# Plain block products for the first feature pair of the SwiGLUs behind the two mixers

## The chip, the cores and the metric

One core of one Trainium2 chip runs the whole program. The metric is the device time of one execution in microseconds (us), median of several runs. The engines are TensorE (PE in the profile; PEld are its weight loads), VectorE (DVE), ScalarE (ACT), GpSimd (POOL) and SyncE (SP), which issues most transfers.

## What is computed

Two layers work on 560 tokens (512 + 32 + 16, feature-major, so a tile is 128 features by tokens). Layer 0 mixes by gated linear attention (GLA), layer 1 by multi-head latent attention (MLA, 544 of the tokens at its end), and each mixer stands between two half-step SwiGLUs:

```python
def swiglu_half(h, norm_w, w_gate, w_up, w_down):
    hn = rmsnorm(h, norm_w)
    return h + 0.5 * ((jax.nn.silu(hn @ w_gate) * (hn @ w_up)) @ w_down)

for i in range(DEPTH):
    h = swiglu_half(h, ffn1_norm[i], ...)
    h = h + mixer_i(rmsnorm(h, mix_norm[i]))      # GLA in layer 0, MLA in layer 1
    h = swiglu_half(h, ffn2_norm[i], ...)
```

The width is 1024, the inner width of a SwiGLU 2816 = 22 tiles of 128 features.

## The kernel before

**Precision.** A float32 operand is split in a high part (`whi`, ScalarE's cast, L371) and a low part (`wlo`, VectorE's subtraction, L372), and a product is three matmuls: high by high (L415), low by high (L416), high by low (L418).

**A pair of feature tiles.** Gate and up of a SwiGLU go over the 22 feature tiles in 11 pairs. A pair is a product of 2 x 2 blocks: the weights of two tiles (each gate and up) by two halves of the input features, times the two halves of the 1024 input features (row blocks 0 to 3 and 4 to 7 of `h`) by the two halves of the tokens (`b11`, `b12`; `b21`, `b22`). Taken plainly this is eight block products of 24 matmuls. `gate_up` does it in seven, in the manner of Strassen and Winograd: it needs sums of the operand blocks (`t4` to `t7`, beside `b11`, `b21` and `b22`) and of the weight quadrants (`Weights.sums`, three additions of 128 x 1024, and one more in the pair; L290), seven splits of weights instead of four, and copies of partial products (L517). The operand sums are made once and serve all pairs of a SwiGLU that use the form. `plain_gate_up` does the eight products. It is used for the first two pairs of the very first SwiGLU (`plain` is 2 there, then 1), where nothing has been made yet: the first of them makes the plain operands, and in the gaps of the second `combine` makes the sums `t4` to `t7`.

**From mixer to SwiGLU.** At each mixer's end stands its output projection: 16 outputs of `ps` (8 row blocks x 2 halves of the tokens, in the order `Quads.ORDER`: for each i the row blocks i and 4 + i of the first half, then of the second), 12 matmuls each, with three banks `ps` in PSUM. VectorE adds each output to `h` (L760 in GLA, L1412 in MLA), which frees the bank. After each addition the object of the coming SwiGLU, a `Quads`, is called with its row block and half: `parts` scales `h` by the norm's weights and splits it (`scaled_parts`, L181 and L182) and makes the operand sums (L192 to L203 and the splits on `t` and `q`), `square` adds up squares for the norm (L213, L217, L220), and at three counts it loads the first pair's weights, splits two quadrants and makes the weight sums (`ahead`). I call these 16 outputs the mixer's tail. Then comes the first pair: banks A, B, C (two PSUM banks each), the norm's roots (`roots2`: matmuls with ones, L467; steps on `ry`, `rt` on VectorE, L482 to L490; transposes, L475), and `finish` for each feature tile and half (multiply by the root, silu, product, split into `ah` and `al`).

**Order.** The code is written in one order, and the framework's scheduler sets each engine's queue from it by its own estimate; engines run their queue in order and wait for each other by semaphores. In what follows an instruction's line is that of the profile, and the changed kernel's lines are higher by 3 ahead of `plain_gate_up` and by 4 to 6 behind it (L290 becomes L293, L598 L602, L760 L765).

Of the kernel before, what the change touches and what calls it, by code (L numbers as in the profile page):

```python
# [33 lines left out]
HALF_T = ((0, T // 2), (T // 2, T))  # L34
HALF_Q = ((0, TQ // 2), (TQ // 2, TQ))
# [60 lines left out]
class Normed(list):  # L96
# [7 lines left out]
    def parts(self, m, hf):  # L104
        net, nc = self.net, self.net.nc
        c = slice(*self.halves[hf])
        if not self:
            self.extend((net.xtile(), net.xtile()) for _ in range(ND))
            self.y = net.np_.tile([P, T], F32, name="yn", tag="yn")
        hm, w = net.h[:, m, c], net.nv[:, self.w0 + m:self.w0 + m + 1]  # L110
        hi, lo = self[m]
        nc.scalar.activation(hi[:, c], hm, AF.Copy, scale=w)
        nc.vector.scalar_tensor_tensor(lo[:, c], hm, w, hi[:, c].bitcast(F32), op0=ALU.mult, op1=ALU.subtract)
# [21 lines left out]
class Quads(Normed):  # L135
# [48 lines left out]
    def parts(self, m, hf):  # L184
        net, nc, n = self.net, self.net.nc, self.n
        v = nc.vector
        i = m % 4
        if hf == 0:
            self.scaled_parts(*self.place("b11" if m < 4 else "b21", i), m, 0)
        elif m < 4:  # L190
            b12, t5 = (self.tmp.tile([P, 280], F32, name=x, tag=x, bufs=1)[:, :n] for x in ("b12", "t5"))
            nc.scalar.activation(b12, self.piece(m, 1), AF.Copy, scale=self.weight(m))  # L192
            v.scalar_tensor_tensor(t5, self.piece(m, 0), self.weight(m), b12, op0=ALU.mult, op1=ALU.subtract)
            net.split(*self.place("t5", i), t5)
            self.kept[i] = b12, t5
        else:
            b12, t5 = self.kept.pop(i)
            q = self.tmp.tile([P, 4, 280], F32, name="q", tag="q", bufs=1)
            b22, t6, t7, t4 = (q[:, j, :n] for j in range(4))
            nc.scalar.activation(b22, self.piece(m, 1), AF.Copy, scale=self.weight(m))  # L200
            v.scalar_tensor_tensor(t6, t5, -1.0, b22, op0=ALU.mult, op1=ALU.subtract)
            v.tensor_tensor(t7, b22, b12, op=ALU.subtract)
            v.scalar_tensor_tensor(t4, self.piece(m, 0), self.weight(m), t6, op0=ALU.mult, op1=ALU.add)  # L203
            self.place("t6", i)
            t = self.sets["t6"][1][i]
            net.split(t[:, 0, :, :n], t[:, 1, :, :n], q[:, :, :n])
# [122 lines left out]
class Net:  # L329
# [238 lines left out]
    def plain_gate_up(self, i, l, f, xs, act, tp, between):  # L568


        nc = self.nc
        v = nc.vector
        n = xs.n
        early = xs.plain == 2
        W, w = xs.first, {}
        xs.first = None
        if W is None:
            W = Weights(self, i, l, f, xs.raws)
            W.load(0, 1, 2, 3)

        def product(to, q, op, more=False):
            if early and not more:
                x = xs.direct(op)
            if q not in w:
                w[q] = self.whole(W.r[q], 2 if early and q == 0 else 1)
            if not early or more:
                x = xs.direct(op)
            for j in range(2):
                self.mm(to[:, j, :n], w[q], 4 * j, x, (0, n), more)
            if early and q < 2:  # L590
                for _ in range(4):
                    Normed.square(xs, op[-1] == "2")

        def finish(j, hf, src):
            gu = tp.tile([P, 2, 280], F32, name="gu", tag="gu", bufs=2)
            t = gu[:, :, :n]
            y = xs.scale(hf).unsqueeze(1).to_broadcast([P, 2, n])
            v.tensor_tensor(t, src[:, :, :n], y, op=ALU.mult)  # L598
            g, u = gu[:, 0, :n], gu[:, 1, :n]
            nc.scalar.activation(g, g, AF.Silu)  # L600
            v.tensor_tensor(g, g, u, op=ALU.mult)
            c = slice(*xs.halves[hf])  # L602
            self.split(act[j][0][:, c], act[j][1][:, c], g)

        def hold(of, tag):
            if not early:
                return of
            r = tp.tile([P, 2, 280], F32, name="r", tag=tag, bufs=1)
            nc.scalar.copy(r[:, :, :n], of[:, :, :n])
            return r  # L610

        done = [0]

        def gap():
            done[0] += 1
            if not early and done[0] <= 4:
                xs.combine(done[0] - 1)
            if done[0] < 8:
                between(done[0])

        held = []
        for (j, hf), bank, tag in zip(((0, 0), (0, 1), (1, 0), (1, 1)), "ACBA", ("ra", "rb", None, None)):
            D = self.bank2(bank)
            for kh in (0, 1):
                product(D, 2 * j + kh, ("b11", "b21", "b12", "b22")[2 * hf + kh], kh == 1)
                if kh == 0:
                    gap()
            held.append((j, hf, hold(D, tag) if tag else D))
            if early and (j, hf) == (0, 1):
                xs.roots()  # L630
            if not early or j:
                for x in held:
                    finish(*x)
                held = []
            gap()
        xs.plain -= 1
# [380 lines left out]
    def softmax(self, pool, p, parts):  # L1017

        nc = self.nc
        st = pool.tile([P, 8], F32, name="st", tag="st", bufs=4)  # L1020
        for i, (s, n, c) in enumerate(parts):
            nc.vector.reduce_max(st[:, i:i + 1], s[:, :n], axis=AX.X)
        if len(parts) == 2:
            nc.vector.tensor_tensor(st[:, 0:1], st[:, 0:1], st[:, 1:2], op=ALU.max)
        nc.vector.tensor_scalar(st[:, 2:3], st[:, 0:1], -SCALE, None, op0=ALU.mult)
        for i, (s, n, c) in enumerate(parts):
            nc.scalar.activation(p[:, c:c + n], s[:, :n], AF.Exp, bias=st[:, 2:3], scale=SCALE,
                                 accum_out=st[:, 3 + i:4 + i])
        if len(parts) == 2:
            nc.vector.tensor_tensor(st[:, 3:4], st[:, 3:4], st[:, 4:5], op=ALU.add)  # L1030
        nc.vector.reciprocal(st[:, 5:6], st[:, 3:4])
        n = sum(q[1] for q in parts)
        nc.vector.tensor_scalar(p[:, :n], p[:, :n], st[:, 5:6], None, op0=ALU.mult)
# [422 lines left out]
def tile_stream_step(ctx: ExitStack, tc: tile.TileContext, a: dict):  # L1456
    nc = tc.nc
    net = Net(ctx, tc, a)
    nc.scalar.dma_start(net.nv, a["nv"])

    def quads(name, halves, side, raws=None):

        if raws is None:
            rp = Pools(tc, side)
            raws = rp, rp(f"raw_{name}", 6)
        x, t = Pools(tc, side), Pools(tc, side)
        xs = Quads(net, name, halves, x("xf"), None if name == "f1_0" else t("xt"), raws[1])
        xs.pools, xs.rp = (x, t), raws
        return xs
# [27 lines left out]
            return mixed[-1][0]  # L1497
        return turn

    def to_quads(xs, name, halves, side, ffn, ahead):  # L1500
        def turn():
            if xs is not None:
                xs.pools[0].close()
            mixed.append(quads(name, halves, side, None if xs is None else xs.rp))
            mixed[-1].ffn, mixed[-1].ahead = ffn, ahead
            return mixed[-1]
        return turn

    mixed = []
# [4 lines left out]
    net.ffn(1, 0, x0, HALF_T, "right", to_mixer(x0, "mix_0", "left", 16, 8))  # L1514
    ys, pools, kept, op = mixed[-1]
    net.psum(False)
    net.gla(ys, to_quads(None, "f2_0", HALF_T, "right", (2, 0), (1, 8, 12)), "left", op, pools)
    kept.close()
    xs = mixed[-1]
    xs.pools[1].close()  # L1520
    net.psum(True)
    net.ffn(2, 0, xs, HALF_T, "left", to_quads(xs, "f1_1", HALF_T, "right", (1, 1), (8, 12, 14)))
    xs = mixed[-1]
    xs.pools[1].close()
    net.ffn(1, 1, xs, HALF_T, "left", to_mixer(xs, "mix_1", "right", 20))
    ys, pools, _, _ = mixed[-1]
    net.psum(False)
    net.mla(ys, to_quads(None, "f2_1", HALF_Q, "left", (2, 1), (1, 8, 12)), "left")
    pools.close()
    xs = mixed[-1]  # L1530
    xs.pools[1].close()
# [165 lines left out]
```

## Time and profile before

| | |
|---|---|
| median of 3 runs | 2053.05 us (2052.42 to 2053.82) |
| the profiled execution | 2054.99 us, of which its span is 2053.1 |
| busy: PE, DVE, ACT | 2006.6, 1619.7, 1009.5 us |
| granted TensorE clock, mean | 0.992 |
| read from HBM | 173.69 MB |
| weight additions L290 | 168, of 1220 ns |
| GLA's tail, first pair behind it | 633.44 to 666.58, 666.58 to 692.53 us of the span |
| MLA's tail, first pair behind it | 1638.0 to 1667.2, 1667.2 to 1691.05 us |

A row of the timeline has start, length, engine, line, operation, output and inputs, shapes and count; brackets hold the idle time ahead of it and what ended it. Durations of neighbours on one engine overlap by some 0.08 us, so the pace is read from start to start. The clock is given as a share of full speed.

### The profile page before, as it was taken

How to read it: one execution, taken by the hardware profiler on the slowest of the kernel's cores; microseconds unless marked ns; L12 is line 12 of the kernel's file. 1: busy time of each engine (PE TensorE's matmuls, PEld its weight loads, DVE VectorE, ACT ScalarE, POOL GpSimd, SP SyncE). 2: the span in 40 equal slices, each digit the busy share in tenths (PEclk: the TensorE clock that was granted, in tenths of full speed). 3: DMA queues.
4: the chain of work that ended last, by engine and by line, in shares of the span. 5: the costliest groups of instructions: out<-in, count | busy, mean ns of one | idle time of the engine just before them, and what ended most of it. 6: DMA issues, size and time to landing. Idle time of an engine off the chain costs nothing.

```text
span 2053.1 us, 38088 instructions
## 1 busy us (share of the span) xinstructions
PE 2006.6 (98%) x15360; PEld 1975.7 (96%) x15360; DVE 1619.7 (79%) x3044; ACT 1009.5 (49%) x1811; POOL 52.6 (3%) x121
## 2 busy tenths in 40 slices
PE   9999999999998999999999999999989999999997
PEld 9999999989998999999999999999989999999997
DVE  8778788566658888788788878786798898887884
ACT  7444445365445544444455444454576565444451
POOL 0000000101110000000000000000110000000000
PEclk9999999999999999999999999999999999999998
DMA  5232322222221232323313323323111413333221
GB/s 181 74 112 83 103 93 79 70 80 70 68 85 60 96 106 78 104 88 104 103 50 100 104 93 93 99 77 97 56 56 48 129 42 106 101 93 108 85 80 56
DMA packets 91904, 180.16 MB, mean 88 GB/s; under 512 B 10240, under 2 KB 21888, under 8 KB 91728
## 3 DMA queue, kind: packets, MB, share of 16 engines
q1 hardware_dynamic: 86688, 171.91, 26.4%
q10 hardware_dynamic: 5040, 5.82, 0.9%
q8 instruction: 121, 1.98, 0.4%
q14 instruction: 55, 0.45, 0.1%
HBM read 173.69 MB, written 3.99 MB: 87 GB/s over the span
## 4 chain that ended last, share of the span: by engine, by line
PE 79%; DVE 13%; DMA 4%; ACT 2%; issue 2%; SPq 0%; POOL 0%; DVEq 0%; ACTq 0%; POOLq 0%
PE Y L418 8%; PE Y L415 8%; PE Y L416 8%; PE A L416 5%; PE A L415 5%; PE A L418 5%; DVE wlo L372 4%; PE ps L415 3%; PE B L416 3%; PE B L418 3%; PE B L415 3%; PE C L418 3%; PE C L416 3%; PE C L415 3%; PE ps L418 3%; PE ps L416 3%
## 5 line engine op out<-in xcount | busy, mean ns | idle before, releaser
L415 PE MATMUL Y<-ah,whi 128*128 128x280 f32 (+1 forms) x1408 | 374.3, 292 | 4.5 <-ACT ah L371 3.7
L416 PE MATMUL Y<-ah,wlo 128*128 128x280 f32 (+1 forms) x1408 | 373.4, 291 | 0.0
L372 DVE TENSOR_TENSOR wlo<-fr,whi 128x1024 fp32r<-128x1024 f32 (+1 forms) x303 | 365.2, 1215 | 9.6 <-ACT whi L371 9.3
L371 ACT CAST whi<-fr 128x1024 fp32r<-128x1024 f32 (+1 forms) x303 | 314.9, 1048 | 101.6 <-PE C L418 40.6
L415 PE MATMUL A<-x,whi 128*128 128x280 f32 (+1 forms) x1056 | 281.6, 292 | 3.6 <-ACT whi L371 3.3
L416 PE MATMUL A<-x,wlo 128*128 128x280 f32 (+1 forms) x1056 | 281.2, 292 | 0.3 <-DVE wlo L372 0.2
L415 PEld LDWEIGHTS Y<-ah,whi 128*128 128x128 f32 x1408 | 265.9, 189 | 5.9 <-ACT ah L371 4.7
L416 PEld LDWEIGHTS Y<-ah,wlo 128*128 128x128 f32 x1408 | 266.8, 190 | 0.0
L650 DVE SCALAR_TENSOR_TENSOR h<-Y,h 128x280 f32<-128x280 f32 (+1 forms) x320 | 141.2, 444 | 159.1 <-PE Y L418 158.4
L372 DVE TENSOR_TENSOR wlo<-raw,whi 128x512 fp32r<-128x512 f32 (+5 forms) x231 | 196.0, 850 | 75.2 <-ACT whi L371 70.5
L371 ACT CAST whi<-raw 128x512 fp32r<-128x512 f32 (+5 forms) x231 | 169.7, 736 | 166.5 <-PE ps L418 48.7
L418 PE MATMUL Y<-al,whi 128*128 128x280 f32 (+1 forms) x1408 | 233.8, 291 | 0.0
L290 DVE TENSOR_TENSOR fr<-fr 128x1024 f32<-128x1024 f32 x168 | 204.9, 1220 | 25.0 <-DMA fr<-W 22.8
L415 PEld LDWEIGHTS A<-x,whi 128*128 128x128 f32 x1056 | 199.7, 189 | 4.3 <-ACT whi L371 3.6
L416 PEld LDWEIGHTS A<-x,wlo 128*128 128x128 f32 x1056 | 199.7, 189 | 0.9 <-DVE wlo L372 0.9
L418 PEld LDWEIGHTS Y<-al,whi 128*128 128x128 f32 x1408 | 200.3, 189 | 0.0
L416 PE MATMUL B<-x,wlo 128*128 128x280 f32 (+1 forms) x704 | 186.4, 291 | 2.4 <-DVE wlo L372 2.4
L415 PE MATMUL B<-x,whi 128*128 128x280 f32 (+1 forms) x704 | 186.6, 290 | 0.0
L415 PE MATMUL C<-x,whi 128*128 128x280 f32 (+1 forms) x688 | 181.9, 290 | 0.0
L416 PE MATMUL C<-x,wlo 128*128 128x280 f32 (+1 forms) x688 | 181.8, 290 | 0.0
L418 PE MATMUL A<-x,whi 128*128 128x280 f32 (+1 forms) x1056 | 178.3, 291 | 0.0
L517 ACT COPY r<-A 128x560 f32<-128x560 f32 (+1 forms) x126 | 78.4, 623 | 165.4 <-PE A L418 163.7
(405 smaller groups left out, 4089.2 us busy)
## 6 DMA issues: line engine op xcount, KB each, us to landing
fr<-W SPq DMA_DIRECT2D x352, 256.0 KB, 3.4
raw<-W SPq DMA_DIRECT2D x80, 512.0 KB, 3.5
raw<-W SPq DMA_DIRECT2D x100, 256.0 KB, 3.0
raw<-W SPq DMA_DIRECT2D x40, 128.0 KB, 2.1
raw<-W SPq DMA_DIRECT2D x4, 384.0 KB, 3.2
h<-xT SPq DMA_DIRECT2D x2, 560.0 KB, 7.8
o_y<-h SPq DMA_DIRECT2D x8, 136.0 KB, 1.8
o_y<-h ACTq DMA_DIRECT2D x8, 136.0 KB, 1.8
```

The costliest lines, as they stand in the source:

```text
L290: self.net.nc.vector.tensor_tensor(r[out], r[x], r[y], op=ALU.add)
L371: self.nc.scalar.copy(hi, src)
L372: self.nc.vector.tensor_tensor(lo, src, hi.bitcast(F32), op=ALU.subtract)
L415: f(hi[:, b0 + k, :], xh[:, c], start=not more and k == 0, stop=False)
L416: f(lo[:, b0 + k, :], xh[:, c], start=False, stop=False)
L418: f(hi[:, b0 + k, :], xl[:, c], start=False, stop=k == n - 1)
L517: nc.scalar.copy(r[:, :, :n], of[:, :, :n])
L650: nc.vector.scalar_tensor_tensor(self.h[:, m, c], Y[:, :n], 0.5, self.h[:, m, c], op0=ALU.mult, op1=ALU.add)
```

## The change

The SwiGLUs behind the two mixers (`f2_0`, `f2_1`) get `plain = 1`: their first pair is done by `plain_gate_up`, as the second pair of the very first SwiGLU is. In the mixer's tail `parts` makes only `b11`, `b21` and `b22`; the operand sums and `b12` move into the pair (`combine` in its gaps 3 to 6, `direct` for `b12`), and the weight sums (`ahead[2]`, now 0) are not made at all. Two quadrants are still split ahead, so `Weights.ready` is used (`w = W.ready`). The roots are taken after the second product, and the first two `finish` wait until after the fourth.

```diff
@@ Quads.parts
+        elif self.plain:
+            if m >= 4:
+                self.scaled_parts(*self.place("b22", i), m, 1)
         elif m < 4:
@@ Net.plain_gate_up
-        W, w = xs.first, {}
-        xs.first = None
+        lead = not xs.finish
+        W, xs.first = xs.first, None
...
+        w = W.ready
...
-            if not early and done[0] <= 4:
-                xs.combine(done[0] - 1)
+            k = done[0] - (3 if lead else 1)
+            if not early and 0 <= k < 4:
+                xs.combine(k)
...
-            if early and (j, hf) == (0, 1):
+            if lead and (j, hf) == (0, early):
                 xs.roots()
-            if not early or j:
+            if not lead or j or (hf and not early):
                 for x in held:
@@ tile_stream_step
-            mixed[-1].ffn, mixed[-1].ahead = ffn, ahead
+            mixed[-1].ffn, mixed[-1].ahead, mixed[-1].plain = ffn, ahead, plain
+            mixed[-1].made.update(("b11", "b21", "b22"))
...
-    net.gla(ys, to_quads(None, "f2_0", HALF_T, "right", (2, 0), (1, 8, 12)), "left", op, pools)
+    net.gla(ys, to_quads(None, "f2_0", HALF_T, "right", (2, 0), (1, 8, 0), 1), "left", op, pools)
...
-    net.mla(ys, to_quads(None, "f2_1", HALF_Q, "left", (2, 1), (1, 8, 12)), "left")
+    net.mla(ys, to_quads(None, "f2_1", HALF_Q, "left", (2, 1), (1, 8, 0), 1), "left")
```

How it moves instructions, at three places of VectorE's queue. The first is the second half of GLA's tail. `h<-ps` are the evictions, `wlo` a weight's low part, `fr` a weight addition, `x`, `t`, `q` the operands and their sums, `acc` the squares. Before:

```order
L290 TENSOR_TENSOR fr<-fr 128x1024
L201 SCALAR_TENSOR_TENSOR q<-t_7848,q 128x280
L202 TENSOR_TENSOR q<-q,b_7847 128x280
L203 SCALAR_TENSOR_TENSOR q<-h,nv,q 128x280
L220 TENSOR_TENSOR acc<-acc,sq_7878 128x280 x2
L290 TENSOR_TENSOR fr<-fr 128x1024
L372 TENSOR_TENSOR x<-q,x 128x1120
L290 TENSOR_TENSOR fr<-fr 128x1024
L760 TENSOR_TENSOR h<-ps,h 128x280 x3
L372 TENSOR_TENSOR wlo<-fr,whi 128x1024
L182 SCALAR_TENSOR_TENSOR x<-h,nv,x 128x280 x2
L193 SCALAR_TENSOR_TENSOR t_7933<-h,nv,b_7932 128x280
```

The same part of the tail now:

```order
L765 TENSOR_TENSOR h<-ps,h 128x280 x3
L182 SCALAR_TENSOR_TENSOR x<-h,nv,x 128x280 x2
L223 TENSOR_TENSOR acc<-acc,sq_7825 128x280 x2
L765 TENSOR_TENSOR h<-ps,h 128x280 x2
L182 SCALAR_TENSOR_TENSOR x<-h,nv,x 128x280
L223 TENSOR_TENSOR acc<-acc,sq_7845 128x280 x2
L182 SCALAR_TENSOR_TENSOR x<-h,nv,x 128x280
L765 TENSOR_TENSOR h<-ps,h 128x280
L182 SCALAR_TENSOR_TENSOR x<-h,nv,x 128x280
L765 TENSOR_TENSOR h<-ps,h 128x280
L375 TENSOR_TENSOR wlo<-fr,whi 128x1024
L223 TENSOR_TENSOR acc<-acc,sq_7895 128x280 x2
```

The sums and the weight additions between the evictions are gone; a weight's low part (the third quadrant's) has come in.

The second place is the end of MLA's last attention head, ahead of its tail. `pTl` and `el` are low parts of attention weights. Before:

```order
L1412 TENSOR_TENSOR h<-ps,h 128x272 x2
L290 TENSOR_TENSOR fr<-fr 128x1024
L372 TENSOR_TENSOR pTl<-s,pTh 128x4x128
L1412 TENSOR_TENSOR h<-ps,h 128x272 x2
L290 TENSOR_TENSOR fr<-fr 128x1024
L372 TENSOR_TENSOR pTl<-s,pTh 128x4x128
L372 TENSOR_TENSOR el<-s,eh 64x128
```

Now:

```order
L1417 TENSOR_TENSOR h<-ps,h 128x272 x2
L375 TENSOR_TENSOR pTl<-s,pTh 128x4x128
L1417 TENSOR_TENSOR h<-ps,h 128x272 x2
L375 TENSOR_TENSOR pTl<-s,pTh 128x4x128
L375 TENSOR_TENSOR el<-s,eh 64x128
```

The two weight additions between the evictions are gone.

The third place is the end of the first pair behind GLA. `gu<-A` reads bank A, in which the next pair's first product is formed as well; `al` is `finish`'s last step. Before, from the last step on `ry` on:

```order
L290 TENSOR_TENSOR fr<-fr 128x1024
L524 SCALAR_TENSOR_TENSOR gu<-A,r 128x560
L528 TENSOR_TENSOR gu<-gu,yn 128x560 x2
L531 TENSOR_TENSOR gu<-gu 128x280
L372 TENSOR_TENSOR wlo<-fr,whi 128x1024
L372 TENSOR_TENSOR al_7980<-gu,ah_7979 128x280
L531 TENSOR_TENSOR gu<-gu 128x280
L526 TENSOR_TENSOR gu<-C,r 128x560
```

Now:

```order
L602 TENSOR_TENSOR gu<-B,yn 128x560
L375 TENSOR_TENSOR x<-xt,x 128x280
L375 TENSOR_TENSOR wlo<-fr,whi 128x1024
L605 TENSOR_TENSOR gu<-gu 128x280
L293 TENSOR_TENSOR fr<-fr 128x1024
L375 TENSOR_TENSOR al_7942<-gu,ah_7941 128x280
L375 TENSOR_TENSOR wlo<-raw,whi 128x256
L293 TENSOR_TENSOR fr<-fr 128x1024 x2
L602 TENSOR_TENSOR gu<-A,yn 128x560
L293 TENSOR_TENSOR fr<-fr 128x1024
```

Before, bank A was read after the fifth of seven products and the next pair took it two products later. Now A holds the pair's last two products, and three weight additions of the next pair stand ahead of the operation that reads it; TensorE's queue has 13 matmuls of the next pair's bank C ahead of its first one of A.

More of the change, by code (lines that the diff above doesn't have):

```diff
@@ L1498, in to_mixer, with to_quads @@
         return turn
-    def to_quads(xs, name, halves, side, ffn, ahead):
+    def to_quads(xs, name, halves, side, ffn, ahead, plain=0):
         def turn():
```

## The prediction

> **What bounds the kernel now.** I read the page first, then the list of who waited for whom on TensorE, then both mixers' ends in the timeline, and last the busy time of those stretches.
>
> ```profile
> span 2053.1 us, 38088 instructions
> PE 2006.6 (98%) x15360; PEld 1975.7 (96%) x15360; DVE 1619.7 (79%) x3044; ACT 1009.5 (49%) x1811; POOL 52.6 (3%) x121
> ```
>
> TensorE (PE) is busy for 2006.6 us of 2053.1: only 46.5 us are idle. A change that adds matmuls can therefore gain only where it removes such idle time, or time at a reduced clock. The rows of TensorE's waits that lie in the changed stretches (line waited for: total us, times, longest):
>
> ```profile
> PE ps L415 <- DVE h L760: 5.7, 2, 3.3
> PE ps L415 <- DVE h L1412: 4.8, 2, 3.3
> ```
>
> L760 and L1412 are VectorE's (DVE's) additions of the output projection to `h`, in the GLA and in the MLA mixer. The matmuls of L415 need a free bank `ps`, of which there are three, and these additions free it. Each stall by itself, in brackets:
>
> ```profile
> 653.71 0.39 PE L415 MATMUL ps<-o,whi 128*128 128x280 f32 x1 [3.30 <-DVE h L760]
> 664.09 0.40 PE L415 MATMUL ps<-o,whi 128*128 128x280 f32 x1 [2.43 <-DVE h L760]
> 1633.96 0.39 PE L415 MATMUL ps<-x,whi 128*128 128x272 f32 x1 [1.53 <-DVE h L1412]
> 1658.06 0.60 PE L415 MATMUL ps<-x,whi 128*128 128x272 f32 x1 [3.28 <-DVE h L1412]
> ```
>
> The stretches, each with its length, busy time (count) of PE, PEld, DVE, ACT, POOL, then the granted clock, DMA share and GB/s: the GLA tail, the first pair after it, the same two for MLA, what follows each of the four stalls, and one stretch of the very first SwiGLU, which I use further down:
>
> ```profile
> 633.44:666.58 33.14, 27.41 (x193) 26.96 (x192) 32.11 (x68) 20.45 (x36) 0.00 (x0) 0.92 0.26 84
> 666.58:692.53 25.95, 25.00 (x189) 24.55 (x189) 23.70 (x44) 13.65 (x22) 0.00 (x0) 0.97 0.26 83
> 1638.00:1667.20 29.20, 25.92 (x192) 25.56 (x192) 25.51 (x56) 17.59 (x29) 0.00 (x0) 0.94 0.02 6
> 1667.20:1691.05 23.85, 23.57 (x188) 23.14 (x187) 23.28 (x45) 16.45 (x27) 0.00 (x0) 1.00 0.29 89
> 653.70:658.00 4.30, 4.29 (x21) 4.29 (x22) 4.28 (x10) 3.07 (x7) 0.00 (x0) 0.60 0.00 0
> 664.00:668.20 4.20, 4.11 (x20) 4.11 (x21) 4.10 (x10) 3.48 (x7) 0.00 (x0) 0.59 0.00 0
> 1658.00:1661.40 3.40, 3.34 (x15) 3.34 (x15) 3.29 (x10) 2.32 (x5) 0.00 (x0) 0.50 0.00 0
> 1634.00:1638.00 4.00, 3.87 (x23) 3.26 (x24) 4.00 (x8) 1.05 (x1) 0.00 (x0) 1.00 0.00 0
> 27.60:34.30 6.70, 6.70 (x55) 6.70 (x54) 6.70 (x24) 4.42 (x11) 0.00 (x0) 1.00 0.60 207
> ```
>
> In the GLA tail VectorE is busy for 32.1 of 33.1 us: there it is the bound, not TensorE. After the three longer stalls the clock is granted at 0.60, 0.59 and 0.50, after the one of 1.53 us at 1.00. What stands in VectorE's queue there:
>
> ```profile
> 661.23 1.32 DVE L372 TENSOR_TENSOR x<-q,x 128x1120 fp32r<-128x1120 f32 x1
> 662.46 1.22 DVE L290 TENSOR_TENSOR fr<-fr 128x1024 f32<-128x1024 f32 x1
> 663.60 1.15 DVE L760 TENSOR_TENSOR h<-ps,h 128x280 f32<-128x280 f32 x3
> 664.85 1.23 DVE L372 TENSOR_TENSOR wlo<-fr,whi 128x1024 fp32r<-128x1024 f32 x1
> ...
> 666.84 0.50 DVE L193 SCALAR_TENSOR_TENSOR t<-h,nv,b 128x280 f32<-128x280 f32 x1
> 667.26 0.80 DVE L220 TENSOR_TENSOR acc<-acc,sq 128x280 f32<-128x280 f32 x2
> 667.98 0.44 DVE L372 TENSOR_TENSOR x<-t,x 128x280 fp32r<-128x280 f32 x1
> ...
> 669.83 0.44 DVE L201 SCALAR_TENSOR_TENSOR q<-t,q 128x280 f32<-128x280 f32 x1
> 670.19 0.45 DVE L202 TENSOR_TENSOR q<-q,b 128x280 f32<-128x280 f32 x1
> 670.55 0.51 DVE L203 SCALAR_TENSOR_TENSOR q<-h,nv,q 128x280 f32<-128x280 f32 x1
> ```
>
> The three evictions at 663.60 (x3), which end the 2.43 us stall, come behind a split of operand sums (L372 on `q`) and an addition of weights (L290). Starts are closer together than durations, so I count from start to start: 1.23 for the split of `q`, 1.14 for a weight addition and, since it lasts as long, for a weight's low part, 0.42 for an operation like L193 (L182 is of its kind), 0.36 for a plain one of 280 columns, 0.72 for the two of L220.
>
> **The change, term by term.**
>
> *Work that leaves VectorE in each tail.* For each of four row blocks: L193 and its low part (0.42 + 0.36), L201, L202, L203 (0.36 + 0.36 + 0.43) and the split (1.23), 3.16 together, four times 12.6 us. Three weight additions, 3 x 1.14 = 3.4. New there are the low parts of `b22` (4 x 0.42 = 1.7) and of the third weight quadrant (1.14). Net it is 13.2 us less. Of the old tail's work VectorE still owed about 1.8 us that stays (two L220 pairs, one eviction) when TensorE went on to the pair. So the new tail asks for 32.1 - 13.2 + 1.8 = 20.7 us of it. What TensorE asks for, from the last four matmuls of successive output blocks, first GLA, then MLA:
>
> ```profile
> 646.64 0.68 PE L418 MATMUL ps<-o,whi 128*128 128x280 f32 x4
> 648.19 0.68 PE L418 MATMUL ps<-o,whi 128*128 128x280 f32 x4
> ...
> 1652.60 0.67 PE L418 MATMUL ps<-x,whi 128*128 128x272 f32 x4
> 1654.11 0.67 PE L418 MATMUL ps<-x,whi 128*128 128x272 f32 x4
> ```
>
> A block of 12 matmuls takes 1.54 us in GLA and 1.51 in MLA; 16 blocks are 24.6 and 24.2 us. 20.7 is below 24.6, so the tail goes over to TensorE's pace. In the new order the longest run ahead of an eviction is a weight's low part, one L182 and one L220 pair, 1.14 + 0.42 + 0.72 = 2.3 us, and three banks give 3 x 1.54 = 4.6 us. I take all three tail stalls as gone: 3.30 + 2.43 + 3.28 = 9.0 us. The slow stretches after them go too: 4.30 x 0.40 + 4.20 x 0.41 + 3.40 x 0.50 = 5.1 us.
>
> [...]
>
> *Weight additions inside MLA's last head.* In MLA two of the three additions do not stand in the tail but earlier, between evictions, and the first waits for its transfer:
>
> ```profile
> 1631.73 1.23 DVE L290 TENSOR_TENSOR fr<-fr 128x1024 f32<-128x1024 f32 x1 [2.07 <-DMA fr<-W]
> ...
> 1633.48 0.78 DVE L1412 TENSOR_TENSOR h<-ps,h 128x272 f32<-128x272 f32 x2
> ```
>
> The evictions at 1633.48 end TensorE's 1.53 us stall. With the addition gone from this place (order above), they are no longer behind a transfer: -1.5 us. Late next there would be the low parts of `pTl`, which stand between the same evictions. MLA's tail proper loses only one addition, and VectorE's 25.5 us there become 25.5 - 12.6 - 1.1 + 2.8 + 1.8 = 16.4, far below 24.2.
>
> *One product more.* Eight products instead of seven: 24 matmuls more per SwiGLU, at 1.54/12 and 1.51/12: 3.1 + 3.0 = +6.1 us, all on the path, since TensorE has no idle time in which to hide them.
>
> *Roots.* A split of 560 columns, the roots' matmuls and the transposes, as they run now:
>
> ```profile
> 29.89 0.74 DVE L372 TENSOR_TENSOR x<-xt,x 128x560 fp32r<-128x560 f32 x1
> 676.98 1.40 PE L467 MATMUL Y<-ones,acc 128*128 128x1 f32 x12
> 685.49 0.87 PE L475 MATMUL Y<-ident,ry 128*128 128x128 f32 x6 [0.82 <-DVE ry L490]
> ```
>
> The roots move ahead of the third product, the transposes behind the fourth. In GLA the transposes waited 0.82 us for `ry`. Now VectorE has ahead of the last `ry`, from the pair's start: about 3.0 left of the tail (the end of a weight's low part, two L220 pairs, an eviction, one L182), four low parts of `b12` (1.7), a weight (1.1), 2.4 of the four `combine`, 7.1 (each 0.42 + 0.36 + 0.36 + 0.36 + 0.65 + 0.43 + 0.36 = 2.94, with 0.65 for the 560 columns, 0.74 less the overlap), and some 1.0 of small operations: 13.9 us. TensorE arrives after four products and the roots, 12.3 + 1.4 = 13.7. I take 0.5 us of waiting in each; the old pairs had 0.82 and a little: no change.
>
> *A new wait: bank A.* The eighth product ends in bank A, which the next pair needs at once. What empties it (L602 of the changed kernel, 0.65) now stands behind three weight additions of the next pair (3.4 us). From the pair's start VectorE has ahead of it: 3.0 + 1.7 + 4 x 2.94 + three weights 3.4 + small ones 1.1 + three L602, three products and three low parts of `finish` (2.0 + 1.1 + 1.1) + 0.3 + 3.4 = 28.9, and 29.5 with itself. TensorE: 24.6 + 1.4 + 0.9 + 0.5 = 27.4, then 13 matmuls of the next pair's bank C that stand ahead of A, 1.7: 29.1. The wait is 0.4 us if VectorE never idles. Trace bounds: 0 (the list of TensorE's waits names no `gu`, though the very first SwiGLU has this handover), and, if VectorE comes to the additions only when the product ends, 3.4 + 0.65 - 1.7 = 2.4, and 1.7 for the clock, as after the 2.43 us stall: 4.1. I take 1.0, near the lower end, since the stretch 27.60:34.30 has the same `combine` work with VectorE busy for 6.70 of 6.70 us. Two SwiGLUs: +2.0.
>
> What else goes costs nothing, since TensorE does not wait for it: three of seven splits of weights in the pair, on ScalarE and VectorE, and the four copies of partial products. They are in the sums above by being left out. The diff touches no load; on SyncE's queue a few loads change places, and the slot of `fr` that `sums` took is free for the next pair's first transfer. I put both at nothing, because no wait of TensorE in these rows ends on a transfer by itself.
>
> Sum: -9.0 - 5.1 - 1.5 + 6.1 + 0 + 2.0 = **-7.5 us**. The profiled execution took 2054.99 us (span 2053.1) and would come to 2047.5; the median of the runs is 1.9 lower, 2053.05, so I predict 2045.5.
>
> **Rivals.**
>
> 1. *Bank A waits its full price*, 4.1 in each instead of 1.0: +6.2, 2051.7. For it: three long additions ahead of the one operation that frees A. Against: the sum above, 0.4.
> 2. *Tails stay late*: one stall like 664.09's remains in each (2.43 + 1.7): +8.2, 2053.7, no change. Against: 20.7 against 24.6 us.
> 3. *Slower.* In the pair, `combine` goes back and forth between ScalarE and VectorE three times for each of four blocks, where the old sums were split in one pass. If each of the 12 exchanges costs VectorE an idle half microsecond, it reaches bank A 6 us later; the wait grows by 6 and the clock takes 1.7 more, 7.7 in each: 2053.05 - 7.5 + 15.4 = 2061.0. It ends slower from 0.35 us per exchange on, where 2 x (12 x 0.35 + 1.7) = 11.8 is above 7.5 + 4.1. Against: 6.70 busy of 6.70 us in the same work.
> 4. *The slow clock stays*: the slow stretches come from something else than these stalls and lie elsewhere afterwards, 5.1 less gained, 2050.6. Against: they follow the three longer stalls at once. [...]
> 5. *More is gained*: no wait for A (-2.0), and the pairs' unnamed gaps go. The old pairs are 25.95 and 23.85; seven products (21.6 and 21.1), roots and transposes (2.3 each), the 0.82 and 0.6 of slow clock that the first one caught leave some 0.6 and 0.4. Together -3.0: 2042.5.
>
> **How the numbers follow.** A difference under about 0.2% (4.1 us) can't be told from none here: faster means below 2048.9, slower above 2057.2. The forecast 0.58; rival 1 0.13, of which a third (one SwiGLU of the two) would still measure as faster; rival 2 0.07; 3 0.07; 4 0.03; 5 0.12. Faster: 0.58 + 0.12 + 0.04 = 0.74; slower 0.07; the rest 0.19. The range reaches from beyond rival 5 to rival 1: 2041.5 to 2051.7.
>
> **What would show it.** In the changed profile TensorE's waits for the evictions are gone or under 0.5 us, the granted clock is 1.00 in both tails, their blocks are 1.54 and 1.51 us apart, the pairs take some 28.7 and 28.1 us (old length, one product, 1.0 for bank A, and in GLA less the slow clock and the shorter wait for `ry`; in MLA a little more of it), and bank A has a new wait of about 1 us on `gu`. I am wrong if a wait for bank A or for `ry` is above 2 us, or if evictions are still waited for.

## The result, and the profile after

The changed kernel took 2043.85 us (median of 4 runs, 2041.99 to 2046.05), the kernel before 2053.03 (4 runs beside it): a ratio of 0.9948, 95% interval 0.9933 to 0.9963. The forecast was 2045.5, 7.5 us of gain; this first measurement gives 9.2 us by the medians. Two later ones of the same kernel (below) gave 0.9927 (0.9913 to 0.9940) and 0.9935 (0.9922 to 0.9947), 15.3 and 13.8 us by the medians. So the gain is larger than I said, and the first measurement stands at its lower end: it lies within the range of 2041.5 to 2051.7, the two later medians (2039.27 and 2039.67) lie just below it. (A ratio leaves disturbed runs out and need not be the quotient of the medians. Where I turn one into us, it is times 2053.)

The profiled execution after took 2041.99 us. First the page, then TensorE's waits (line waited for: total us, times, longest):

```profile
span 2040.2 us, 38174 instructions
PE 2006.2 (98%) x15408; PEld 1976.2 (97%) x15408; DVE 1603.3 (79%) x3046; ACT 1003.8 (49%) x1821; POOL 52.5 (3%) x121
```

```profile
PE Y L418 <- ACT ah L374: 2.4, 3, 1.7
...
PE A L418 <- DVE gu L602: 1.7, 2, 1.0
...
PE B L419 <- DVE wlo L375: 0.5, 2, 0.3
```

TensorE is as busy as before with 48 matmuls more, and idle for 34.0 us (span less busy) instead of 46.5. The list of after has no row for the evictions (L765, L1417) and none for `ry` at the transposes (L478). The new row is the one for bank A. Three rows of the same list before, which the prediction did not show, matter below:

```profile
PE Y L415 <- ACT ah L371: 3.7, 2, 3.3
...
PE B L416 <- DVE wlo L372: 2.4, 4, 1.0
...
PE Y L475 <- DVE ry L490: 1.0, 2, 0.8
```

The stretches after, in the order GLA tail, pair, MLA tail, pair (length, then busy time and count of PE, PEld, DVE, ACT, POOL, the granted clock, DMA share, GB/s):

```profile
637.79:662.55 24.76, 24.76 (x192) 24.59 (x192) 20.22 (x50) 14.23 (x26) 0.00 (x0) 1.00 0.54 175
662.55:689.66 27.11, 27.00 (x212) 26.77 (x211) 27.11 (x65) 17.81 (x39) 0.00 (x0) 1.00 0.06 21
1628.84:1653.34 24.50, 24.49 (x194) 24.13 (x192) 17.84 (x42) 12.95 (x22) 0.00 (x0) 1.00 0.17 49
1653.34:1679.43 26.09, 26.09 (x213) 26.04 (x211) 26.02 (x64) 18.73 (x40) 0.00 (x0) 1.00 0.06 21
```

Both tails go at TensorE's pace at full clock: 24.76 of 24.76 us busy where it was 27.41 of 33.14. In the pairs VectorE (third of the busy times) hardly rests, 27.11 of 27.11 and 26.02 of 26.09 us. Tail and pair together say why the change works: before, VectorE had 32.11 + 23.70 = 55.8 us of work in a place where TensorE at full clock needs about 48.5 (tail 24.6, seven products 21.6, roots and transposes 2.3); now it has 47.3 and TensorE 51.8. The work was not only moved; by the eight products it became less, and TensorE's more.

In MLA the same sums are closer, 48.8 against 47.6 before (now 43.9 against 50.6), so the sum alone does not account for a stall of 3.28 us there. What stands at each of the three tail stalls is a long run of VectorE's work without an eviction. MLA's begins and ends with

```profile
1650.64 1.22 DVE L372 TENSOR_TENSOR wlo<-fr,whi 128x1024 fp32r<-128x1024 f32 x1
1657.57 1.13 DVE L1412 TENSOR_TENSOR h<-ps,h 128x272 f32<-128x272 f32 x3
```

and is 6.9 us long, where three banks give 3 x 1.51 = 4.5. GLA's are 7.0 and 6.5 us (from 646.16 and from 657.10). After the change the longest run in either tail is 2.3 us, as the prediction said.

Bank A, in TensorE's queue and in VectorE's:

```profile
692.18 0.40 PE L418 MATMUL A<-x,whi 128*128 128x280 f32 x1 [0.67 <-DVE gu L602]
```

```profile
688.99 2.48 DVE L293 TENSOR_TENSOR fr<-fr 128x1024 f32<-128x1024 f32 x2
691.39 0.73 DVE L602 TENSOR_TENSOR gu<-A,yn 128x560 f32<-128x560 f32 x1
```

The operation that frees A starts right behind the weight additions, as forecast.

### The profile page after: what moved, and what is told of

The parts are those of the page before. It is cut to its first block, busy times and chain, and to the rows that moved or that the text cites. A ratio compares the mean times of both kernels' runs of the same rounds, so it can differ in the third digit from the quotient of the medians.

```text
span 2040.2 us, 38174 instructions
## 1 busy us (share of the span) xinstructions
PE 2006.2 (98%) x15408; PEld 1976.2 (97%) x15408; DVE 1603.3 (79%) x3046; ACT 1003.8 (49%) x1821; POOL 52.5 (3%) x121
## 4 chain that ended last, share of the span: by engine, by line
PE 81%; DVE 12%; ACT 3%; DMA 2%; issue 1%; POOL 0%; SPq 0%; DVEq 0%; ACTq 0%; POOLq 0%
PE Y L421 8%; PE Y L418 8%; PE Y L419 8%; PE A L418 5%; PE A L419 5%; PE A L421 5%; PE ps L418 4%; PE ps L421 4%; PE ps L419 3%; DVE wlo L375 3%; PE B L419 3%; PE B L421 3%; PE B L418 3%; PE C L421 3%; PE C L419 3%; PE C L418 3%
## 5 line engine op out<-in xcount | busy, mean ns | idle before, releaser
L375 DVE TENSOR_TENSOR wlo<-fr,whi 128x1024 fp32r<-128x1024 f32 (+1 forms) x297 | 357.8, 1214 | 11.3 <-ACT whi L374 10.6
L374 ACT CAST whi<-fr 128x1024 fp32r<-128x1024 f32 (+1 forms) x297 | 308.5, 1048 | 103.4 <-PE C L421 39.6
L293 DVE TENSOR_TENSOR fr<-fr 128x1024 f32<-128x1024 f32 x160 | 195.1, 1219 | 18.3 <-DMA fr<-W 15.7
L418 PE MATMUL C<-x,whi 128*128 128x280 f32 (+1 forms) x672 | 177.5, 290 | 0.0
L419 PE MATMUL C<-x,wlo 128*128 128x280 f32 (+1 forms) x672 | 177.5, 290 | 0.0
```

What stands on the lines that cost most here:

```text
L293: self.net.nc.vector.tensor_tensor(r[out], r[x], r[y], op=ALU.add)
L374: self.nc.scalar.copy(hi, src)
L375: self.nc.vector.tensor_tensor(lo, src, hi.bitcast(F32), op=ALU.subtract)
L418: f(hi[:, b0 + k, :], xh[:, c], start=not more and k == 0, stop=False)
L419: f(lo[:, b0 + k, :], xh[:, c], start=False, stop=False)
```

## The experiments

**The same kernels again.** No edit.

> The changed kernel once more, unchanged, for a second profile. Theory 1 (the gain is the stalls' length; a half-clock stretch is a lottery of 1.7 us each): 2042 to 2046 us again, and the profile again without waits for evictions, but with a different number or place of half-clock stretches than 4 (two at the start, two near 436). Theory 2 (half-clock stretches belong to fixed waits): the same stretches at the same places, and runs no further apart than 1.5 us.

> The changed kernel a third time, since its first measurement gave 9.2 us and the second 15.3 us under the kernel before. Theory 1 (waits gone or come: -9.0 in the tails, -1.2 in MLA's last head, +6.1 for the products, +1.7 for bank A, -0.8 for the roots, some -3 of transfers no longer held up in f2_0 and f1_1, and three to four half-clock stretches of 1.7 us less on average): 12 us under the kernel before, 10 to 15. Theory 2 (the first measurement was right, the second had a lucky kernel): 9 us or less. Its profile has waits for A of 0.7 and 1.0 us and none above 0.5 for B between 690 and 1130 us.

> The kernel before once more, for a second profile. Theory 1 (waits belong to the program, within 0.3 us; half-clock stretches follow where TensorE is busy for less than about half of one of the 3.41 us of a fixed grid, so they depend on where the grid lies): the same waits at the same places, with the 3.3 us ones followed by a half-clock stretch again, and the one of 2.4 us in three of four cases. Theory 2 (stretches belong to the program): the same seven stretches.

Measured: the first 2039.27 us (6 runs) against 2054.53 (13), under the 2042 to 2046 that I expected; the second 2039.67 (5) against 2053.51 (9), within its 10 to 15; the kernel before once more 2055.9 (1 run). The pages of the three, in this order:

```profile
span 2034.7 us, 38174 instructions
PE 2001.8 (98%) x15408; PEld 1973.0 (97%) x15408; DVE 1602.5 (79%) x3046; ACT 1003.5 (49%) x1821; POOL 52.4 (3%) x121
```

```profile
span 2037.9 us, 38174 instructions
PE 2006.2 (98%) x15408; PEld 1977.2 (97%) x15408; DVE 1603.1 (79%) x3046; ACT 1003.7 (49%) x1821; POOL 52.4 (3%) x121
```

```profile
span 2054.0 us, 38088 instructions
PE 2009.3 (98%) x15360; PEld 1977.9 (96%) x15360; DVE 1619.3 (79%) x3044; ACT 1010.6 (49%) x1811; POOL 52.6 (3%) x121
```

With the records of the clock, this splits each span in three. A half-clock stretch stands there as 3413 ns at 0.5 (seven times before) or as 6827 ns (twice after), which I count as two; by my estimate, 3.41 x 0.50, it costs 1.7 us where TensorE is busy all through it (the ones at the end, around and behind its last matmuls, are not counted):

| | idle (span less PE) | half-clock stretches x 1.7 | the rest |
|---|---|---|---|
| before | 46.5 | 7: 11.9 | 1994.7 |
| before, again | 44.7 | 9: 15.3 | 1994.0 |
| after | 34.0 | 4: 6.8 | 1999.4 |
| after, again | 32.9 | 0 | 2001.8 |
| after, third | 31.7 | 3: 5.1 | 2001.1 |

On average 12.7 us less idle time, 9.6 less at half clock, and 6.4 more work, which are the two products (forecast 6.1): 15.9 in all between the profiles. The mechanism of theory 1 holds in all three: the waits for evictions are gone in each profile of after and stand in both of before, and the number and places of the stretches change from run to run. Waits above 0.35 us mostly come back at the same place within 0.3 us (3.30, 2.43 and 3.28 us in the tails of both profiles of before); those that transfers set do not (1.0 and 0.8 us for B at 745 and 1127 us in one, a single one of 1.6 in the other; below). Between two runs of one kernel TensorE's matmuls shift almost only where one run has a half-clock stretch and the other does not: the profiles "after" and "after, again" drift 1.8 us apart in the first 96 us and 3.0 at 436 to 443, where the first had two stretches each, and under 1 us in all the rest.

**When the clock halves.** In the traces of before and after every record of the clock but the last, which the program's end cuts off, is a whole number of 3.413 us long, from 1 (the stretches at half) to 466, so the stretches of one execution lie on one grid. Its start differs between executions: a cell begins at 654.48 us before and at 665.02 before, again, 10.54 us or 3.09 cells apart. Two neighbours of the grid in the kernel before, around the 3.30 us stall; then the same 1.8 us wait in MLA's beginning (a wait for `vl`, untouched by the change) in the run with GLA alone and in the run with MLA alone:

```profile
651.07:654.48 3.41, 0.77 (x6) 0.77 (x7) 3.41 (x6) 1.14 (x3) 0.00 (x0) 1.00 0.00 0
654.48:657.89 3.41, 3.41 (x16) 3.41 (x16) 3.39 (x8) 2.18 (x6) 0.00 (x0) 0.50 0.00 0
```

```profile
1483.04:1486.45 3.41, 1.59 (x14) 1.34 (x12) 3.24 (x12) 2.65 (x6) 2.11 (x5) 1.00 0.01 2
1486.45:1489.86 3.41, 3.41 (x15) 3.41 (x14) 2.87 (x11) 2.37 (x9) 0.00 (x0) 0.50 0.38 112
```

```profile
1487.35:1490.76 3.41, 1.86 (x16) 1.60 (x14) 3.21 (x9) 3.26 (x8) 2.32 (x6) 1.00 0.01 2
1490.76:1494.17 3.41, 3.15 (x23) 3.15 (x24) 3.36 (x15) 1.78 (x7) 0.00 (x0) 1.00 0.12 29
```

With TensorE busy for 0.77 or 1.59 of 3.41 us the next cell ran at 0.50; with 1.86 it ran at 1.00. I cut all 14 profiles between 460 and 2000 us in this way, with matmuls and weight loads as busy time: of 30 cells under half busy, 29 were followed by a half-clock cell, of 76 between 0.505 and 0.75, five. Six more followed a cell over 0.75 busy that itself ran at half clock; each is the second of two in a row. Ahead of 460 us the count does not tell it as well: cells with TensorE busy for 2.81 and 2.71 of 3.41 us (from 412.14 before and from 432.89 after) were followed by one at 0.50. My estimate, from half of the 3.41 us and these counts: a stall of 3.3 us nearly always costs 1.7 more, one of 2.4 us in about three of four positions of the grid, and one under 1.7 us alone hardly ever. So it is a draw in each run. It goes with the spread of one kernel's runs, which lie up to 10 us apart (the kernel before: 2051.4 to 2061.2 in one comparison of 29 runs): the six of them with a mean granted clock of 0.993 took 2053.0 us on average, the five with 0.988 or 0.989 took 2059.6. It also goes with the small gain of the first measurement: its four runs of after had 0.9940 on average, the later ones 0.9958 and 0.9950. One stretch is 0.0008 of the mean (1.7 of 2053 us), so these are two and one stretches, 3.7 and 2.0 us, of the 4.6 and 4.2 us between the medians.

**GLA alone, MLA alone.** One of the two calls is put back:

```diff
-    net.mla(ys, to_quads(None, "f2_1", HALF_Q, "left", (2, 1), (1, 8, 0), 1), "left")
+    net.mla(ys, to_quads(None, "f2_1", HALF_Q, "left", (2, 1), (1, 8, 12)), "left")
```

> Plain first pair in f2_0 only; f2_1 as before. Theory 1, by the prediction's terms for GLA (3.30 + 2.43 + 3.4 of clock gained, 3.1 for the product and 1.0 for bank A lost): 5.0 us faster than before, 2048.0; by the two profiles' steps from 442 to 745 us, 7.4 faster, 2045.7. Theory 2 (part of the gain comes from outside the two tails, at 1002 us and at the end): less than 4 us faster, 2049 or more, and the two single changes do not add up to the whole.

> Plain first pair in f2_1 only; f2_0 as before. Theory 1, by the prediction's terms for MLA (1.5 of the last head, 3.28 + 1.7 gained, 3.0 and 1.0 lost): 2.5 us faster, 2050.5; by the two profiles' steps 4 us faster, 2049. Theory 2 (the end of the program gains by itself, whatever stands before it): over 5 us faster. The GLA tail keeps its two waits of about 3.3 and 2.4 us.

Measured: GLA alone 2044.51 us, ratio 0.9949 (0.9935 to 0.9963), 10.5 us; MLA alone 2049.73, 0.9977 (0.9964 to 0.9990), 4.7 us. The sum, 15.2, is the whole (15.0 in the same comparison). That speaks against theory 2 for GLA; for MLA theory 2 asked for over 5 us, and the interval (2.1 to 7.4 us) does not exclude it. TensorE's waits between 600 and 1135 us, GLA alone and then MLA alone:

```profile
PE Y L418 <- ACT ah L374: 2.1, 1, 2.1
PE A L418 <- DVE gu L602: 0.7, 1, 0.7
PE B L419 <- DVE wlo L375: 0.3, 1, 0.3
```

```profile
PE ps L418 <- DVE h L765: 4.9, 2, 3.3
PE B L419 <- DVE wlo L375: 2.1, 2, 1.1
```

Each part was worth about twice what I gave it (5.0 and 2.5). The waits for B, at 745 and 1127 us of the kernel before, come and go with f2_0's first pair, though they lie two pairs behind it and in the next SwiGLU.

**What moved the waits for B.** Matmuls of one column in the warm-up of the kernel before:

```diff
         nc.tensor.matmul(warm[:, :P], net.ones, net.ones, start=True, stop=True)
+    for _ in range(24):
+        nc.tensor.matmul(warm[:, :1], net.ones, net.ones[:, :1], start=True, stop=True)
```

> The kernel before with 24 matmuls of one column more in the warm-up at the start, in TensorE's idle time there (3.3 us); nothing else is changed. They move TensorE's instruction stream by 48 instructions, as one more product does. Theory 1 (blocks of 16 KB of instructions are fetched every 256 instructions of TensorE and hold up the weight transfer that they meet by over 1 us; the change moved them off the transfers that the waits for B at 745 and 1127 us and for ah at 1002 us hang on): these waits, 1.0, 0.8 and 3.3 us before, are gone or, at 1002, under 2.2, with no plain product in the kernel, and the time is 2 to 4 us below before. Theory 2 (these waits went because f2_0's first pair is another one, by the slot of fr or by VectorE's lag): they stay as they were, no difference or up to 1 us slower. The waits for ps in both tails stay in both theories.

Measured: 2058.1 us, ratio 1.0012 (1.0000 to 1.0024), so not faster. The mechanism is seen, the time was forecast wrongly. VectorE before and with the 24 matmuls, at the additions that the wait at 745 us hangs on:

```profile
740.09 2.48 DVE L290 TENSOR_TENSOR fr<-fr 128x1024 f32<-128x1024 f32 x2 [2.73 <-DMA fr<-W]
```

```profile
741.26 2.49 DVE L290 TENSOR_TENSOR fr<-fr 128x1024 f32<-128x1024 f32 x2 [1.09 <-DMA fr<-W]
```

And the transfers issued in those 4 to 5 us, before (735.3 to 740.1) and with the matmuls (KB each, median us from issue to landing):

```profile
q8 instruction: 1, 0.02, 1.8%
...
fr<-W SPq DMA_DIRECT2D x2, 256.0 KB, 3.8
```

```profile
fr<-W SPq DMA_DIRECT2D x2, 256.0 KB, 2.9
```

Before, a packet of 16384 bytes of instructions (queue q8) falls in the transfer's flight, and that transfer landed after 4.65 us; in the run with the matmuls, without the packet, it took 3.01. (I take the queue for TensorE's: 30,720 matmuls and weight loads over its 121 packets are 254 each, and with the semaphore instructions of TensorE's queue 256 lie between two packets on average, in the traces of before and of after.) In the changed kernel the fetch came some 3 us earlier in the pair and met two transfers that nobody waited for (4.6 us each in "after, again"), and VectorE's wait for the needed one was 1.44. It is so in all 14 profiles: the four with the old pair and no matmuls added have the fetch on the needed transfer (4.65 to 5.5 us) and waits for B of 1.0 to 1.9, the others neither (3.0 to 3.7 us; in one a fetch ends 0.2 us after the issue). At 1127 us it is the same, except that one of those four escapes. At 1742 us (0.5) it was not the transfer waited for that met a fetch, but the one issued two ahead of it. This does not hold for every transfer: of the 256 KB transfers to `fr` in the 14 profiles, the 1177 with a fetch in their flight took 3.6 us in the median, the 3751 without 3.3, so where a fetch costs over 1 us depends on more than its presence. At 745 and 1127 us, where a transfer was due just in time, TensorE waited 1.0 and 0.8 us for B before.

The time did not follow. First, the row of the added matmuls:

```profile
5.76 7.27 PE L1515 MATMUL Y<-ones 128*128 128x1 f32 x48
```

Each of the 24 runs as two, so the stream moved twice as far as I had meant (the fetch comes some 6 us earlier, not 3), and they took 7.3 us, 3.5 beyond TensorE's idle time there. Second, the shifted fetches met others: new waits for `ah` of 0.9 us at 1384 and 1.2 at 1995. The wait at 1002 us was 2.8, not under 2.2; it was 1.8 in the second profile of before without any edit, so at most a part of it is of this cause.

**Sums of weights in the pair.** `ahead` is (1, 8, 0) in the kernel before, without `plain`:

> The kernel before, seven products, with the three weight additions of both SwiGLUs made in the first pair instead of ahead of it (ahead is 1, 8, 0). Theory 1 (tails go by VectorE's sum of work): in GLA 3.4 us less of VectorE in the tail, so of the 5.7 us of stalls some 2.5 stay; in MLA the stall of 1.53 in the last head goes, the tail (25.5 less 1.1 against 24.2) keeps 2 of 3.3; the pair has 3.4 more on VectorE and waits 1 to 2 us in it: 4 us faster than before. Theory 2 (only the operand sums hold up the tails): 1.5 us faster at most, and the stalls of 3.3 us stay in both tails. Theory 3 (the additions stop the third product, whose weight they make): 2 us or more slower.

Measured: 2054.08 us, ratio 0.9997 (0.9986 to 1.0009): no change. The row between 600 and 1135 us and the one between 1600 and 1760:

```profile
PE ps L415 <- DVE h L760: 3.3, 1, 3.3
PE B L415 <- ACT whi L371: 2.1, 1, 2.1
```

```profile
PE ps L415 <- DVE h L1412: 4.7, 2, 3.3
```

By the time this is theory 2, but the run does not tell the theories apart, since the edit did not do what I meant: the scheduler put the additions into the tails and into MLA's last head again (the first of MLA's is at 1636.33 between evictions, behind 1.91 us of waiting for its transfer). Only the 2.43 us stall of GLA went, and came back as 2.1 us for B in the pair: a stall moved, not removed.

**The load put back.** Nine subtractions behind each `b22` of GLA in the changed kernel, and in a second version four:

```diff
             if m >= 4:
                 self.scaled_parts(*self.place("b22", i), m, 1)
+                if n == 280:
+                    for _ in range(9):
+                        d = self.tmp.tile([P, 280], F32, name="b12", tag="b12", bufs=1)[:, :n]
+                        v.tensor_tensor(d, self.piece(m, 1), self.piece(i, 1), op=ALU.subtract)
```

> The changed kernel with 36 subtractions of 128 x 280 (0.36 us each, 13 us) put into VectorE's queue in GLA's tail, nine behind each of the last four row blocks' low parts; their results are not used. Theory 1 (the tail's stalls are VectorE's load alone, whatever it does): about what the operand sums and weight additions were (13.2 us), so waits for ps of 4 to 6 us in GLA's tail come back, with one or two half-clock stretches, and the time is 6 to 9 us above the changed kernel. Theory 2 (the stalls came from where the splits of 1120 columns and the weight additions stood, long operations ahead of evictions; short ones fit between): waits under 2 us, 0 to 3 us above the changed kernel.

> As the run with 36 subtractions in GLA's tail, with 16 of them (5.8 us). By sums: tail and first pair together held 47.6 us of VectorE's work in 52.1 us of TensorE's time, so 4.5 us are free, and the load goes 1.3 over. Theory 1 (tail and pair have one budget): waits of 1 to 3 us in all in GLA's tail and pair, no wait above 1.7 us and so no half-clock stretch there: 1 to 3 us above the changed kernel. Theory 2 (the tail has a budget of its own, 24.6 against 20.7 + 5.8 = 26.5): a wait for ps of about 2 us, with a half-clock stretch in half of the runs: 2 to 4 above. Theory 3 (every extra operation in the tail delays an eviction): 5 or more.

Measured: nine 2051.44 us, ratio 0.9983 (0.9974 to 0.9993), 3.5 us under before and so, by the ratios of the changed kernel elsewhere, some 10 above it (expected: 6 to 9); four 2042.92, 0.9948 (0.9933 to 0.9963), 2.7 above the changed kernel in the same comparison. Waits between 600 and 1135 us with nine, then with four:

```profile
PE ps L422 <- DVE h L769: 2.8, 1, 2.8
...
PE B L423 <- DVE wlo L379: 1.3, 2, 0.9
PE Y L482 <- DVE ry L497: 1.0, 1, 1.0
PE A L423 <- DVE wlo L379: 0.7, 1, 0.7
PE B L422 <- ACT whi L378: 0.6, 1, 0.6
```

```profile
PE ps L422 <- DVE h L769: 1.0, 1, 1.0
PE Y L482 <- DVE ry L497: 0.8, 1, 0.8
PE A L422 <- DVE gu L606: 0.6, 1, 0.6
```

Load brings the waits back, without a sum or a split in it. But I had the full load's waits in the tail (4 to 6 us); there were 2.8 for `ps` and 3.6 behind it, in the pair, so what the tail does not pay the pair pays. With four, 5.8 us in 4.5 free ones, the waits are 2.4 us against 0.7, as theory 1 of that run had them; its 2.7 us lie within theory 2's range too, and are not clear of noise.

The runs do not show that the amount alone makes the stalls in the tail, since the scheduler also stacked the load between evictions, and each wait for `ps` ends such a run. Longest run without an eviction, then the wait at its end: before 7.0 and 3.30, 6.5 and 2.43 (1.61 in the run with MLA alone), in MLA 6.9 and 3.28; with nine subtractions 5.7 and 2.76, with four 3.35 and 1.03; after 2.3 and none. In the run with the weight sums in the pair, GLA's 7.0 us run kept its stall of 3.3, while the other run had shrunk from 6.5 to 3.4 and had none. No run keeps the load and spreads it evenly, and none puts a load back in MLA, so how much the amount does and how much the order stays open.

**The wait for A.** The last two products go into bank C:

```diff
-        for (j, hf), bank, tag in zip(..., "ACBA", ("ra", "rb", None, None)):
+        for (j, hf), bank, tag in zip(..., "ACBC" if lead and not early else "ACBA", ("ra", "rb", None, None)):
```

> The changed kernel with the pair's last two products in bank C instead of A, so that the next pair's first product in A finds its bank free and C is asked for 24 matmuls later. Theory 1 (the wait for A, 0.7 and 1.0 us, is a delay on the path and nothing waits for something else in its place): both waits gone, 1.7 us faster than the changed kernel, 2042.1 in the median. Theory 2 (VectorE is behind at that place and TensorE waits for it a little later): the wait comes back on C or on a weight's low part, no difference. Theory 3 (the seventh product waits for C, which VectorE empties late): over 1 us slower.

> The last two products in bank C once more, beside the changed kernel on the same chip. Theory 1: 1.7 us under the changed kernel (the two waits for A), 1 to 3. Theory 2 (the first difference of 1.5 was chance): within 0.5 of the changed kernel.

Measured: 2037.76 and 2038.25 us, ratios 0.9918 (0.9905 to 0.9931) and 0.9928 (0.9916 to 0.9940), 1.5 and 1.4 us under the changed kernel beside each. The intervals of the two kernels overlap, but both times the difference is the size of the waits, and the waits are gone; between 1600 and 1760 us this is all that is left:

```profile
PE C L418 <- DVE gu L602: 0.2, 1, 0.2
```

Theory 1. This is the fastest version that I ran.

**Where a plain pair does not pay.** The same in the SwiGLU that follows f2_0 without a mixer between:

```diff
-    ... to_quads(xs, "f1_1", HALF_T, "right", (1, 1), (8, 12, 14)))
+    ... to_quads(xs, "f1_1", HALF_T, "right", (1, 1), (8, 12, 0), 1))
```

> The version with the last products in bank C, and a plain first pair also in f1_1, whose rows are summed not in a mixer's tail but in the last down projection of f2_0, where TensorE does 25 of 25 us and VectorE 21. Theory 1 (a plain pair pays only where VectorE has more work than TensorE in the stretch of tail and pair; otherwise it costs its 24 matmuls): 3.1 us slower than without it, 2 to 5. Theory 2 (a plain pair is better after every handover, since it lets the sums go into the pair): no slower, or faster.

Measured: 2044.15 us, ratio 0.9957 (0.9944 to 0.9969), against 0.9928 without it: 6.0 us slower, one more than the 2 to 5 expected. The pair in both, without and with:

```profile
1041.66:1065.31 23.65, 23.65 (x188) 23.65 (x187) 21.95 (x41) 13.65 (x22) 0.54 (x1) 1.00 0.27 90
```

```profile
1043.20:1070.02 26.82, 26.82 (x212) 26.82 (x211) 25.93 (x63) 17.01 (x37) 0.54 (x1) 1.00 0.06 20
```

3.17 us for 24 matmuls, with TensorE busy throughout: theory 1, and the price of a product by itself. Of the other 2.8, a new wait for `ah` of 0.7 at 1376 us stands in the profile, and two more half-clock stretches, at 439 and 1487 us; the first lies ahead of the edit's place, so it is a draw. The rest stays open within the intervals.

## Why the forecast was right in its direction and too small

In the terms of the table above, the forecast was 8.5 us less idle time, 5.1 less at half clock and 6.1 more work; the profiles have 12.7, 9.6 and 6.4. The first two are too small, by some 4 us each.

*Tail stalls, -9.0.* Right: 3.30, 2.43 and 3.28 in both profiles of before, none after. Rival 2 falls. The estimate of VectorE's work in GLA's tail was 20.7 us, the trace has 20.2 (MLA 16.4 and 17.8).

*Half clock behind them, -5.1.* Right as far as it goes: three stretches in the tails in both profiles of before, none after. Rival 4 falls. What I missed is that a stretch followed nearly every cell under half busy (29 of 30), so that other stalls draw too. The remaining difference of the averages (5.6 stretches instead of 3) is one stretch at 1002 us in both profiles of before, and draws; over all runs on record the mean clocks, 0.991 in 51 runs before and 0.995 in 15 after, make it about five.

*MLA's last head, -1.5.* Right: 1.53 and 1.14 before, none after.

*Products, +6.1.* Right: 6.4 by the table, 3.17 for one.

*Roots, 0.* Wrong by 0.9 (0.8 in GLA, the rest in MLA): I expected `ry` to be late by 0.5 us again in each. My sums were 13.9 for VectorE and 13.7 for TensorE from the pair's start; the trace has 13.95 and 14.0, so `ry` was just in time:

```profile
676.34 0.16 DVE L493 SCALAR_TENSOR_TENSOR ry<-rt,ry 128x6 f32<-128x6 f32 x1
```

```profile
676.55 0.65 PE L478 MATMUL Y<-ident,ry 128*128 128x128 f32 x4
```

*Bank A, +2.0.* Right: 0.67 and 1.01, three profiles alike. The count for GLA, 29.5 us of VectorE and 29.1 of TensorE, met 29.6 and 29.0. Rival 1 (4.1 each) falls, and rival 3 too: VectorE had no idle time between `combine`'s exchanges.

*"What else goes costs nothing", the step that failed.* I put the changed loads at nothing because no wait of TensorE ended on a transfer by itself. But VectorE's additions ended on one, and B on them: 2.3 and 2.1 us in the two profiles of before (745, 1127 and 1742 us), 0 to 0.5 after. At 745 and 1127 us the 48 instructions that the longer pair adds to TensorE's stream moved the fetches off the transfers needed; for 1742 us this is argued. The wait for `ah` at 1002 us, 3.3 and 1.8 before and 1.4 to 1.7 after, differs as much between the two profiles of before as between them and after, so its 1.0 is in part chance. These some 3.2 us of idle time come from when transfers land, not from less work on VectorE. That they are worth it in time is not shown, since the run with added matmuls moved the fetches and was no faster (it also lost 3.5 us at its start).

Idle time by these terms: -9.0 - 1.3 - 0.9 + 1.7 - 2.2 - 1.0 = -12.7, as in the table. The pairs themselves took 27.1 and 26.1 us, with A 27.8 and 27.1. The forecast had 28.7 and 28.1, and its own terms for GLA add up to 29.1 (25.95 + 3.1 + 1.0 - 0.6 - 0.3), so they were some 1 us shorter each than forecast: the roots' wait, and the old pairs' unnamed gaps, which rival 5 had named.

## What to carry to other kernels

Add up what each engine has to do over the whole stretch in which the work can be moved (here GLA's tail and pair, 55.8 us of VectorE against 48.5 of TensorE), not stage by stage: where the helper engine's sum was the larger, plainer arithmetic on the full engine paid; where it wasn't, it cost its matmuls, 3.2 us. Then look for the longest run of the helper's work between two operations that the full engine waits for (here 6.5 to 7.0 us against three banks' 4.6). A stall is to be priced with what the clock does after it (here 0.50 to 0.60 behind the three in the tails, 5.1 us on top of their 9.0). And a gain measured once over four runs can be off by half its size (9.2 us here, then 15.3 and 13.8) when runs draw half-clock stretches: look at where two runs of one kernel differ before comparing two kernels.

## What the hardware showed beyond this

- TensorE's clock went down by whole cells of 3.413 us, of a grid that lay differently from execution to execution (3413 or 6827 ns at 0.5 in the records of before and after). Between 460 and 2000 us of the 14 profiles, the cell behind one under half busy ran at 0.50 in 29 of 30 cases, behind one from 0.505 to 0.75 in 5 of 76.
- Of the 256 KB weight transfers, the two followed above took 4.4 to 5.5 us with a packet of 16 KB of instructions in their flight (3.6 once, where it came at the very end) and 3.0 to 4.0 without it or with its end only. Over all such transfers the median goes only from 3.3 to 3.6. Which transfer a packet met moved with the number of TensorE's instructions ahead of it: 24 matmuls more at 5.76 us changed waits at 745, 1384 and 1995 us.
